# A two-layer encoder in split fp32: when ScalarE is asked for the second silu of a seven-product chunk and for the high parts of pair sums

## The chip, the core and the metric

The kernel runs on one core of a Trainium2 chip. The metric is the device time of one execution in microseconds (us); the core works on batch 1, 256 tokens, model width 1024.

## What is computed

Two layers, each `x += 0.5*SwiGLU(norm(x)); x += Mixer(norm(x)); x += 0.5*SwiGLU(norm(x))`, then a last RMSNorm. Layer 0 mixes with global and windowed attention, layer 1 with neighbourhood attention. The change touches only the four SwiGLU blocks:

```python
def swiglu(h, w_gate, w_up, w_down):          # h: 256 x 1024, d_ff = 2816
    return (jax.nn.silu(h @ w_gate) * (h @ w_up)) @ w_down
```

All in float32.

## The kernel before

Every fp32 operand of a product is split into a high part (fp32r, written by ScalarE: `high_part`, L474) and a low part (the rest, written by VectorE: `low_part`, L477). A "product" is then three TensorE matmuls (L466 to L468): high by high, low by high, high by low. Weights come in 1 MB loads into three rotating `raw` tiles; a load is asked for on the SP queue (L376) as soon as the low part of the last piece of an earlier load is asked for. Split weights live in seven `hi`/`lo` pairs (`wp`).

The four SwiGLU blocks are called stages 0, 2, 3 and 5. In each, d_ff is worked in five chunks of 512 columns and one of 256. Usually gate and up are two runs of eight products for each half (`tt`) of the 256 tokens. One or two chunks in each stage (table `SEVEN`, six in all) replace eight products by seven for some row pairs (Strassen's scheme over 2 x 2 blocks: two halves of the tokens by gate and up). Their results lie in seven or eight PSUM banks (`M["1"]`, `"5"`, `"6"`, `"7"`, `"00"`, `"01"`, `"10"`, `"11"`), and VectorE adds them up (`common`, `first_gate`, `rest` in `seven_gates`): `first_gate` gives the first half's gate and its silu (L785); `rest` gives the first half's up, then the second half's gate (L802) and its silu (L804), the second half's up (L805, L808) and the product of the two (L789, `up`).

Each finished 128 x 512 product of gate and up (`glu`) is turned by `transposed`: ScalarE copies it into two planes (L551), SP issues a transposing DMA (L553), ScalarE copies it back (L555), and the high and low parts `g_h`, `g_l` are made for the down product. Fifteen pairs of rows of the down product (the `s` entries in `DOWN`) are done by the seven-product scheme as well. For these, `quarters` copies pieces of the turned product (L696, L699) into a tile called `quarters`, which has one buffer, VectorE forms sums (L702, and L709, L710 in `sums_of`), and their high and low parts are called `k<f>h` and `k<f>l`, with `f` twice the pair's number.

Every engine takes its instructions in the order in which the Python code asks for them; no scheduler reorders them. The order of side work comes from generators: each `yield n` means "go on n products later", counted by `tick`, which runs after each product that TensorE is asked for. Supplying one more split weight (`supply`) is also counted there. So a number in a `yield` sets how many products', and thereby how many weights', instructions stand ahead on each queue.

Of the kernel before, what the change touches and what calls it, by code (L numbers as in the profile page):

```python
# [13 lines left out]
AF = mybir.ActivationFunctionType  # L14
# [39 lines left out]
R_WAIT = 3  # L54
GLU_WAIT = 6
TURN_WAIT = [1, 16]
NAT_WAIT = 2
ROPE_WAIT = [3, 3]
KB_WAIT = {
# [143 lines left out]
class Trunk:  # L203
# [343 lines left out]
    def turned_over(self, m, w):  # L547
# [3 lines left out]
        self.nc.scalar.copy(planes.rearrange("p (h c) -> p h c", h=2), back.rearrange("p (c h) -> p h c", h=2))  # L551
        yield TURN_WAIT[0]
        self.nc.sync.dma_start_transpose(back.rearrange("p (j t) -> p j t", t=P), planes)  # L553
        yield TURN_WAIT[1]
        self.nc.scalar.copy(planes.rearrange("p (c h) -> p h c", h=2), back.rearrange("p (h c) -> p h c", h=2))  # L555
# [98 lines left out]
    def ffn(self):  # L654
        nc = self.nc
# [19 lines left out]
        def transposed(tt, f0, w, m):  # L675
            n = w // P
            tb = yield from self.turned_over(m, w)
            pairs = [f for f in range(f0, f0 + n) if f in paired and f + 1 < f0 + n]
            parts = []
            for f in pairs:  # L680
                yield from quarters(tt, f, tb, f - f0)

            if tt == 1 and f0 + n - 2 in pairs:
                n -= 1
            yield from self.split_psum(tb, n, f"g{tt}_{f0}_", parts)
            for j, part in enumerate(parts):
                gT[tt][f0 + j] = part
            for f in pairs if tt == 1 else []:
                yield from sums_of(f)
# [16 lines left out]
        def sums_of(f):  # L706

            k = paired[f]
            nc.vector.tensor_tensor(k[:, 1, :], k[:, 2, :], k[:, 1, :], op=ALU.subtract)  # L709
            nc.vector.tensor_tensor(k[:, 0, :], k[:, 1, :], k[:, 0, :], op=ALU.add)  # L710
            yield 1
            hi, lo = (self.t([P, 4, P], f"k{f}{p}", 1, F32R) for p in "hl")
            self.high_part(hi, k)
            yield 1
            self.low_part(lo, k, hi)
            sums[f] = [(hi[:, i, :], lo[:, i, :]) for i in (3, 2, 1, 0)]

# [33 lines left out]
        def seven_gates(f0, w, pairs7):  # L751

            while len(K) < 4:
                self.tick(False)
            self.rate = SEVEN_RATE[self.now.n]
            h, M, c = self.now.hT, {}, {}
            op = nc.vector.tensor_tensor

            def copy():
                yield 1  # L760
                c["m"] = self.t([P, 512], "glu", 3)
                nc.scalar.activation(c["m"], M["1"], AF.Copy)

            def common():

                yield 1
                while "m" not in c:
                    yield 1
                w = self.t([P, 512], "silu", 2)
                op(w, M["6"], c["m"], op=ALU.add)  # L770
                yield 1
                y = self.t([P, 512], "glu", 3)
                op(y, M["5"], w, op=ALU.subtract)
                yield 1
                nc.vector.scalar_tensor_tensor(w, M["7"], -1.0, w, op0=ALU.mult, op1=ALU.add)
                c["y"], c["w"] = y, w

            def first_gate():
                yield 1
                while "m" not in c:  # L780
                    yield 1
                s = self.t([P, 512], "silu", 2)
                op(s, M["00"], c["m"], op=ALU.add)
                yield 1
                nc.scalar.activation(s, s, AF.Silu, scale=self.now.r[0])  # L785
                c["s"] = s

            def up(tt, o, u, s):
                nc.vector.scalar_tensor_tensor(o, u, self.now.r[tt], s, op0=ALU.mult, op1=ALU.mult)  # L789
                self.spawn(transposed(tt, f0, w, o), GLU_WAIT)  # L790
                yield 1

            def rest():
                yield 1
                while "s" not in c or "w" not in c:
                    yield 1
                y, z, m = c["y"], c["w"], c["m"]
                op(y, M["01"], y, op=ALU.add)
                yield 1
                tasks.append(self.start(up(0, y, y, c["s"])))  # L800
                yield 1
                op(m, M["10"], z, op=ALU.add)  # L802
                yield 1
                nc.scalar.activation(m, m, AF.Silu, scale=self.now.r[1])  # L804
                op(z, M["5"], z, op=ALU.subtract)  # L805
                yield 1
                if "11" in M:
                    op(z, M["11"], z, op=ALU.add)  # L808
                    yield 1
                tasks.append(self.start(up(1, m, z, m)))  # L810

            def product(name, lh, piece, first, last):
                self.mm(M[name], lh, piece, first, last)

            n7 = KD // 2 - pairs7
            M.update((name, self.bank(tag)) for name, tag in [("00", "s"), ("01", "s"), ("10", "s")])
            if n7:
                M["11"] = self.bank("o")
            for q in range(KD // 2):
                k, first, last = 2 * q, q == n7, q == KD // 2 - 1  # L820
                if q < n7:
                    pieces = self.take(4)
                    for i in range(2):
                        for n, piece in enumerate(pieces[2 * i : 2 * i + 2]):
                            for tt in range(NT):
                                product(f"{tt}{n}", h[tt][k + i], piece, k + i == 0, tt == n == 1 and i == 1 and q + 1 == n7)
                    continue
                b11, b21, b22, t7, t5, t8, t6 = self.take(7)
                if first:
                    for task in tasks:  # L830
                        self.finish(task)
                    M.update((name, self.bank(tag)) for name, tag in [("1", "pj"), ("5", "pj"), ("7", "tp")])
                    M["6"] = self.bank("tp" if n7 else "o")
                j = q - (KD // 2 - most)
                product("1", h[0][k + 1], b11, first, last)
                if last:
                    self.start(copy())
                product("00", h[0][k], b21, q == 0, last)
                if last:
                    tasks.append(self.start(first_gate()))  # L840
                product("01", K[0][j], b22, q == 0, last)
                product("7", K[3][j], t7, first, last)
                product("5", K[2][j], t5, first, last)
                product("10", h[1][k], t8, q == 0, last)
                product("6", K[1][j], t6, first, last)
            self.start(common())
            tasks.append(self.start(rest()))

        f0 = 0
# [456 lines left out]
    def odd(self, rel):  # L1306
# [11 lines left out]
        def natural(i, tt, ps, dst):  # L1318
# [7 lines left out]
            nc.scalar.activation(nat, ps, AF.Copy, scale=rs[tt] if i == 0 else r)  # L1326
            yield NAT_WAIT
            tb = self.turned(nat)
# [234 lines left out]
```

## Time and profile before

| | |
|---|---|
| median of 3 runs | 964.62 us (964.39 to 965.56) |
| the profiled execution | 964.38 us, span of its core 962.6 us |
| mean granted TensorE clock | 0.989 |
| busy: TensorE, VectorE, ScalarE, GpSimd | 931.9, 791.1, 676.4, 91.9 us |
| weight load (beside TensorE's matmuls) | 757.2 us |
| HBM | 177 GB/s over the span |

In the profile, PE is TensorE's matmul, PEld its weight load, DVE VectorE, ACT ScalarE, POOL GpSimd, SP the queue that issues the loads. A row reads `output<-inputs`, with buffer numbers left out. A bracket at the end of a timeline row gives the time that the engine stood idle ahead of it and what ended most of that. Times are from the start of the span.

### The profile page before, as it was taken

To read this page: it belongs to the slowest core of one execution; us is meant where nothing else is said; L and a number is where in the kernel's file an instruction comes from. 1 tells how busy PE (TensorE), PEld (TensorE's weight loads), DVE (VectorE), ACT (ScalarE), POOL (GpSimd) and SP (SyncE) were. 2 spreads that over 40 slices of the span, in tenths; PEclk is the share of its full clock that TensorE was granted. 3 is DMA by queue.
4 is the path that set the end of the run, shared out by engine and by line. 5 is a ranking of instruction groups with operands and counts; after the bars stand their busy time and mean duration, and the time that the engine had idled before them with its cause. 6 is when DMAs were issued, how large, how long until landed. Compare 5 with 4: busy or idle time off the path is not lost.

```text
span 962.6 us, 12408 instructions
## 1 busy us (share of the span) xinstructions
PE 931.9 (97%) x4399; PEld 757.2 (79%) x4399; DVE 791.1 (82%) x1228; ACT 676.4 (70%) x1091; POOL 91.9 (10%) x152
## 2 busy tenths in 40 slices
PE   9999999999999999999999989899999999999997
PEld 6887888877788787887887768688778788878885
DVE  6799688778879988688978887888777787986898
ACT  7687885567787686774766758647777687767763
POOL 1300000064410000000100000006130000000001
PEclk9999999999999999999999999899999999999999
DMA  8857876553246675867557567564543448477751
GB/s 298 277 153 247 263 213 215 182 138 88 89 132 197 219 213 181 244 204 262 175 141 239 171 209 225 199 242 126 174 133 131 132 144 272 121 257 218 224 208 56
DMA packets 129343, 183.16 MB, mean 190 GB/s; under 512 B 50688, under 2 KB 63744, under 8 KB 129280
## 3 DMA queue, kind: packets, MB, share of 16 engines
q1 hardware_dynamic: 128704, 181.58, 59.8%
q8 instruction: 34, 0.56, 0.2%
q10 hardware_dynamic: 576, 0.79, 0.2%
q14 instruction: 29, 0.24, 0.1%
HBM read 169.76 MB, written 1.05 MB: 177 GB/s over the span
## 4 chain that ended last, share of the span: by engine, by line
PE 48%; DVE 26%; ACT 14%; issue 6%; DMA 4%; POOL 0%; SPq 0%; POOLq 0%; ACTq 0%; DVEq 0%
DVE lo L477 10%; PE pj L466 7%; PE pj L468 7%; PE pj L467 7%; ACT hi L474 6%; PE s L467 6%; PE s L468 6%; PE s L466 5%; DVE raw L392 2%; DMA glu<-turned 2%; DVE two L392 2%; ACT turned L555 2%; DVE slo L477 2%; PE o L1035 2%; DVE g_l L477 1%
## 5 line engine op out<-in xcount | busy, mean ns | idle before, releaser
L477 DVE TENSOR_TENSOR lo<-raw,hi 128x1024 fp32r<-128x1024 f32 (+1 forms) x372 | 376.5, 1030 | 100.8 <-ACT hi L474 99.6
L474 ACT ACTIVATE hi<-raw 128x1024 fp32r<-128x1024 f32 (+1 forms) x372 | 317.6, 889 | 47.7 <-PE s L468 17.8
L467 PE MATMUL s<-lo,th 128*128 128x512 f32 x373 | 146.7, 393 | 7.9 <-DVE lo L477 7.8
L466 PE MATMUL s<-hi,th 128*128 128x512 f32 x373 | 147.0, 394 | 3.1 <-ACT hi L474 1.5
L466 PE MATMUL pj<-hi,th 128*128 128x512 f32 x367 | 147.0, 401 | 0.0
L467 PE MATMUL pj<-lo,th 128*128 128x512 f32 x367 | 143.8, 392 | 2.4 <-DVE lo L477 2.3
L468 PE MATMUL s<-hi,tl 128*128 128x512 f32 x373 | 145.9, 391 | 0.0
L468 PE MATMUL pj<-hi,tl 128*128 128x512 f32 x367 | 143.4, 391 | 0.0
L467 PEld LDWEIGHTS s<-lo,th 128*128 128x128 f32 x373 | 70.2, 188 | 25.4 <-DVE lo L477 11.5
L466 PEld LDWEIGHTS s<-hi,th 128*128 128x128 f32 x373 | 70.2, 188 | 19.4 <-ACT hi L474 3.3
L467 PEld LDWEIGHTS pj<-lo,th 128*128 128x128 f32 x367 | 69.2, 189 | 16.8 <-DVE lo L477 4.0
L468 PEld LDWEIGHTS s<-hi,tl 128*128 128x128 f32 x373 | 70.3, 188 | 14.4
L466 PEld LDWEIGHTS pj<-hi,th 128*128 128x128 f32 x367 | 69.3, 189 | 14.5 <-issue 0.9
L468 PEld LDWEIGHTS pj<-hi,tl 128*128 128x128 f32 x367 | 69.0, 188 | 14.6
L486 POOL TENSOR_TENSOR rstd<-var,mhalf 128x1 f32<-128x1 f32 (+2 forms) x16 | 17.1, 1070 | 613.5 <-ACT th L507 328.9
L555 ACT COPY turned<-glu 128x1024 uint16<-128x1024 uint16 (+1 forms) x48 | 60.1, 1253 | 10.3 <-DMA glu<-turned 10.3
L468 PE MATMUL s<-hi,g_l 128*128 128x512 f32 (+1 forms) x131 | 51.8, 396 | 3.7 <-DVE g_l L477 3.7
L551 ACT COPY turned<-glu 128x1024 uint16<-128x1024 uint16 (+1 forms) x48 | 46.2, 964 | 9.7 <-DVE glu L672 7.3
L466 PE MATMUL s<-hi,g_h 128*128 128x512 f32 (+1 forms) x131 | 52.1, 398 | 0.0
L467 PE MATMUL s<-lo,g_h 128*128 128x512 f32 (+1 forms) x131 | 51.3, 392 | 0.0
L474 ACT ACTIVATE shi<-two 128x1024 fp32r<-128x1024 f32 x30 | 31.7, 1055 | 27.0 <-DVE two L392 27.0
L477 DVE TENSOR_TENSOR slo<-raw,shi 128x1024 fp32r<-128x1024 f32 x30 | 36.6, 1220 | 11.1 <-ACT shi L474 11.1
(483 smaller groups left out, 1685.8 us busy)
## 6 DMA issues: line engine op xcount, KB each, us to landing
raw<-in_ffn_w_down SPq DMA_DIRECT2D x44, 1024.0 KB, 5.2
raw<-in_ffn_w_up SPq DMA_DIRECT2D x28, 1024.0 KB, 5.2
raw<-in_ffn_w_gate SPq DMA_DIRECT2D x26, 1024.0 KB, 5.2
raw<-in_ffn_w_gate SPq DMA_DIRECT2D x35, 512.0 KB, 4.0
raw<-in_ffn_w_up SPq DMA_DIRECT2D x32, 512.0 KB, 5.0
raw<-in_odd_w_qkv SPq DMA_DIRECT2D x12, 1024.0 KB, 5.1
raw<-in_even_w_in SPq DMA_DIRECT2D x4, 1024.0 KB, 5.2
raw<-in_even_w_out SPq DMA_DIRECT2D x8, 512.0 KB, 5.9
```

Source lines behind the costliest of these rows:

```text
L392: add = lambda o, x, y: self.nc.vector.tensor_tensor(o, x, y, op=ALU.add)
L466: mm(ps, h, wh, start=first, stop=False)
L467: mm(ps, h, wl, start=False, stop=False)
L468: mm(ps, l, wh, start=False, stop=last)
L474: self.nc.scalar.activation(hi, src, AF.Copy)
L477: self.nc.vector.tensor_tensor(lo, src, hi.bitcast(F32), op=ALU.subtract)
L486: nc.gpsimd.tensor_tensor(r[:, :n], v[:, :n], self.mhalf[:, :n], op=ALU.pow)
L551: self.nc.scalar.copy(planes.rearrange("p (h c) -> p h c", h=2), back.rearrange("p (c h) -> p h c", h=2))
L555: self.nc.scalar.copy(planes.rearrange("p (c h) -> p h c", h=2), back.rearrange("p (h c) -> p h c", h=2))
L1035: self.nc.tensor.matmul(O[64 * s : 64 * s + 64, i * P : i * P + P], v(b0 + i, s, kc), pT[s][:, i, kc, :], start=(kc == 0), stop=(kc == 1),)
```

## The change

Two lists of waits are new. In `sums_of` the high part of a pair sum is asked for six products after VectorE's sums, and the low part two after that; it was one and one. In `first_gate` the first silu is asked for three products after VectorE's sum instead of one. In `rest` the second silu (L804 before, L811 now) moves from one product behind its sum to behind the second half's up sums and four products more, and the product of the two comes another two products later.

```diff
+SUMS_WAIT = [6, 2]
+SILU_WAIT = [3, 4, 2]
...
         def sums_of(f):
...
             nc.vector.tensor_tensor(k[:, 0, :], k[:, 1, :], k[:, 0, :], op=ALU.add)
-            yield 1
+            yield SUMS_WAIT[0]
             hi, lo = (self.t([P, 4, P], f"k{f}{p}", 1, F32R) for p in "hl")
             self.high_part(hi, k)
-            yield 1
+            yield SUMS_WAIT[1]
             self.low_part(lo, k, hi)
...
                 op(s, M["00"], c["m"], op=ALU.add)
-                yield 1
+                yield SILU_WAIT[0]
                 nc.scalar.activation(s, s, AF.Silu, scale=self.now.r[0])
...
                 op(m, M["10"], z, op=ALU.add)
                 yield 1
-                nc.scalar.activation(m, m, AF.Silu, scale=self.now.r[1])
                 op(z, M["5"], z, op=ALU.subtract)
                 yield 1
                 if "11" in M:
                     op(z, M["11"], z, op=ALU.add)
-                    yield 1
+                yield SILU_WAIT[1]
+                nc.scalar.activation(m, m, AF.Silu, scale=self.now.r[1])
+                yield SILU_WAIT[2]
                 tasks.append(self.start(up(1, m, z, m)))
```

TensorE's and GpSimd's rows stand in the same order as before; on SP, at two places, a transposing DMA of a second half stands behind one weight load more. Lines below the new lists are numbered two or three higher in the changed kernel (L474 becomes L476, L804 becomes L811). Three places of the order follow.

ScalarE in stage 2, chunk 3 (the seven-product chunk whose second silu ran at 379.99 us); `hi<-raw` rows are weights, `silu_37xx` the first silu, `glu_3718` the second, `turned` the copies for turning. Before:

```order
L785 ACTIVATE silu_3731<-silu_3731,rstd_2940 128x512
L474 ACTIVATE hi_3740<-raw_3605 128x1024
L474 ACTIVATE k10h_3750<-quarters_3670 128x512
L474 ACTIVATE hi_3757<-raw_3695 128x1024
L474 ACTIVATE hi_3770<-raw_3695 128x1024
L474 ACTIVATE hi_3791<-raw_3711 128x1024
L804 ACTIVATE glu_3718<-glu_3718,rstd_3030 128x512
L667 ACTIVATE silu_3812<-pj_3764,rstd_2940 128x512
L551 COPY turned_3821<-glu_3780 128x1024
L474 ACTIVATE hi_3823<-raw_3711 128x1024
L474 ACTIVATE hi_3836<-raw_3747 128x1024
L551 COPY turned_3846<-glu_3718 128x1024
```

and in the changed kernel:

```order
L476 ACTIVATE hi_3739<-raw_3600 128x1024
L787 ACTIVATE silu_3731<-silu_3731,rstd_2940 128x512
L476 ACTIVATE hi_3753<-raw_3695 128x1024
L476 ACTIVATE hi_3766<-raw_3695 128x1024
L476 ACTIVATE k10h_3781<-quarters_3670 128x512
L476 ACTIVATE hi_3790<-raw_3711 128x1024
L669 ACTIVATE silu_3810<-pj_3760,rstd_2940 128x512
L553 COPY turned_3819<-glu_3776 128x1024
L476 ACTIVATE hi_3821<-raw_3711 128x1024
L811 ACTIVATE glu_3718<-glu_3718,rstd_3030 128x512
L476 ACTIVATE hi_3835<-raw_3746 128x1024
L476 ACTIVATE hi_3846<-raw_3746 128x1024
```

The first silu moved behind one weight's high part, k10's high part behind two more, and the second silu from ahead of the next chunk's first silu (`silu_38xx`) to behind it, the first half's turning copy and one more high part; the second half's turning copy left this stretch.

ScalarE in stage 3, where the second half of the first seven-product chunk is copied back and its pair sum k6 is split; `shi` rows are the high parts of weights of seven-product pairs. Before:

```order
L555 COPY turned_5032<-glu_4910 128x2x512
L551 COPY turned_5132<-glu_5083 128x1024
L699 ACTIVATE quarters_5104<-turned_5032 128x128
L474 ACTIVATE g_4_h_5147<-turned_5032 128x384
L474 ACTIVATE shi_5152<-two_5116 128x1024
L474 ACTIVATE k6h_5165<-quarters_5104 128x512
L474 ACTIVATE shi_5168<-raw_5015 128x1024
L474 ACTIVATE hi_5178<-raw_5041 128x512
L474 ACTIVATE hi_5189<-raw_5041 128x1024
L551 COPY turned_5199<-glu_5150 128x1024
L474 ACTIVATE shi_5201<-two_5185 128x1024
```

and in the changed kernel:

```order
L553 COPY turned_5131<-glu_5083 128x1024
L476 ACTIVATE shi_5146<-two_5116 128x1024
L476 ACTIVATE shi_5156<-raw_5013 128x1024
L557 COPY turned_5061<-glu_4910 128x2x512
L476 ACTIVATE hi_5166<-raw_5039 128x512
L701 ACTIVATE quarters_5104<-turned_5061 128x128
L476 ACTIVATE hi_5178<-raw_5039 128x1024
L476 ACTIVATE g_4_h_5186<-turned_5061 128x384
L553 COPY turned_5195<-glu_5144 128x1024
L476 ACTIVATE shi_5197<-two_5173 128x1024
L476 ACTIVATE k6h_5220<-quarters_5104 128x512
```

The copy back of `glu_4910` moved behind two `shi` rows, and k6's high part from ahead of a chunk's last `shi` to behind the first `shi` of the next load.

ScalarE in stage 3's down product, around the pair sum k16. Before:

```order
L474 ACTIVATE hi_5669<-raw_5511 128x512
L699 ACTIVATE quarters_5625<-turned_5560 128x128
L474 ACTIVATE g_16_h_5685<-turned_5560 128x512
L474 ACTIVATE k16h_5697<-quarters_5625 128x512
L474 ACTIVATE hi_5700<-raw_5511 128x1024
L555 COPY turned_5610<-glu_5572 128x2x256
L474 ACTIVATE shi_5718<-two_5676 128x1024
```

and in the changed kernel:

```order
L476 ACTIVATE hi_5669<-raw_5511 128x512
L701 ACTIVATE quarters_5625<-turned_5556 128x128
L476 ACTIVATE g_16_h_5685<-turned_5556 128x512
L476 ACTIVATE hi_5697<-raw_5511 128x1024
L557 COPY turned_5610<-glu_5568 128x2x256
L476 ACTIVATE shi_5714<-two_5676 128x1024
L476 ACTIVATE k16h_5722<-quarters_5625 128x512
```

k16's high part moved behind a weight's high part, a copy back and one `shi`.

## Prediction

> **What bounds the kernel now.** First the page (busy time by engine), then the list of waits, which says who keeps whom waiting (total us, times, longest).
>
> ```profile
> PE 931.9 (97%) x4399; PEld 757.2 (79%) x4399; DVE 791.1 (82%) x1228; ACT 676.4 (70%) x1091; POOL 91.9 (10%) x152
> ...
> ACT glu L804 <- DVE glu L802: 30.4, 6, 6.2
> ...
> PE s L467 <- DVE lo L477: 7.8, 8, 2.0
> ...
> ACT k16h L474 <- DVE quarters L710: 10.8, 3, 4.2
> ```
>
> TensorE (PE) is busy 97% of the span, so the most that a new order can return are its few gaps. The longest of them end with a low part of a weight (`lo`, L477), which VectorE makes out of the high part from ScalarE. ScalarE meanwhile stands 30.4 us at the six second silus (L804), some 5 us each, for VectorE's sum at L802. These ScalarE waits cost nothing by themselves; what counts is whether the weights queued behind them come late. I name the six chunks with seven products by the time of their L804: A 84.61, B 333.77, C 379.99, D 517.86, E 568.21, F 853.81. The timeline around A shows the chain (start, duration, in brackets the idle time and what ended it):
>
> ```profile
> 84.61 0.72 ACT L804 ACTIVATE glu<-glu,rstd 128x512 f32<-128x512 f32 x1 [5.51 <-DVE glu L802]
> ...
> 88.79 1.23 DVE L477 TENSOR_TENSOR lo<-raw,hi 128x1024 fp32r<-128x1024 f32 x1 [0.58 <-ACT hi L474]
> ...
> 88.64 0.40 PE L468 MATMUL s<-hi,tl 128*128 128x512 f32 x1
> 88.87 0.44 PE L466 MATMUL s<-hi,th 128*128 128x512 f32 x1
> 90.07 0.50 PE L467 MATMUL s<-lo,th 128*128 128x512 f32 x1 [0.76 <-DVE lo L477]
> ```
>
> ScalarE stood 5.51 us, its next high parts came late, VectorE waited for one of them (0.58), and TensorE for the low part. Matmuls start 0.23 us apart when nothing is missing (88.64, 88.87); here the next started after 1.20, so TensorE lost 0.97, which is the bracket plus 0.2. I use "bracket plus 0.2" below.
>
> **The change, chunk by chunk.** No instruction is added or taken away and TensorE's order is the same. On ScalarE the second silu (0.72) and the first one move behind later high parts; the second half's last product (L789, 0.75) moves behind one or two low parts on VectorE; its turning copy, its transposing DMA and its copy back follow some 2 to 4 us later; the high and low parts of the pair sums move behind three to six products' worth of weights.
>
> *A.* The high parts that stood behind L804 now stand ahead of it, so VectorE's idle 0.58 goes and L789 (0.75) stands behind the low part: it is 1.3 us early against a wait of 0.97. Gain 1.0.
>
> *B.* TensorE waits for nothing there; no gain. The cover is that its low parts were in time already; were it gone, one wait like A's, 1.0, would come.
>
> *C.* Two waits of TensorE lie here.
>
> ```profile
> 379.99 0.72 ACT L804 ACTIVATE glu<-glu,rstd 128x512 f32<-128x512 f32 x1 [5.84 <-DVE glu L802]
> 382.12 2.00 ACT L474 ACTIVATE hi<-raw 128x1024 fp32r<-128x1024 f32 x2
> ...
> 370.81 1.23 DVE L477 TENSOR_TENSOR lo<-raw,hi 128x1024 fp32r<-128x1024 f32 x1 [0.75 <-ACT hi L474]
> 381.51 0.75 DVE L789 SCALAR_TENSOR_TENSOR glu<-silu,rstd,glu 128x512 f32<-128x512 f32 x1
> 383.21 2.36 DVE L477 TENSOR_TENSOR lo<-raw,hi 128x1024 fp32r<-128x1024 f32 x2 [0.95 <-ACT hi L474]
> ...
> 372.09 0.51 PE L467 MATMUL pj<-lo,th 128*128 128x512 f32 x1 [0.76 <-DVE lo L477]
> 383.24 0.49 PE L466 MATMUL s<-hi,th 128*128 128x512 f32 x1 [0.19 <-ACT hi L474]
> 384.49 0.50 PE L467 MATMUL s<-lo,th 128*128 128x512 f32 x1 [0.76 <-DVE lo L477]
> ```
>
> At 372.09 the low part waited 0.75 for a high part queued behind the first silu. That silu now stands one high part later, so 0.75 of the 0.97 comes back. At 383.24 and 384.49 TensorE lost 0.35 and 0.97. The low part there is now early by the idle 0.95, L789's 0.75 and the 0.75 from above, 2.45 in all, while TensorE comes at most 0.75 earlier; both waits go. Gain 0.75 + 1.3 = 2.1.
>
> *D and E, one stage.* This is the largest term, and here a later wait takes part of the gain back.
>
> ```profile
> 522.37 0.50 PE L467 MATMUL s<-lo,th 128*128 128x512 f32 x1 [0.77 <-DVE lo L477]
> 547.64 0.50 PE L467 MATMUL s<-lo,th 128*128 128x512 f32 x1 [1.86 <-DVE lo L477]
> 551.85 0.63 PE L467 MATMUL s<-slo,th 128*128 128x512 f32 x1
> 565.92 0.47 PE L466 MATMUL s<-hi,th 128*128 128x512 f32 x1 [1.49 <-DVE glu L798]
> 571.45 0.50 PE L466 MATMUL s<-hi,th 128*128 128x512 f32 x1 [1.17 <-ACT hi L474]
> 572.71 0.71 PE L467 MATMUL s<-lo,th 128*128 128x512 f32 x1 [0.76 <-DVE lo L477]
> 618.02 0.80 PE L468 MATMUL s<-hi,g_l 128*128 128x512 f32 x1 [3.69 <-DVE g_l L477]
> ...
> 539.83 0.63 ACT L474 ACTIVATE k6h<-quarters 128x512 fp32r<-128x512 f32 x1 [3.59 <-DVE quarters L710]
> 568.21 0.73 ACT L804 ACTIVATE glu<-glu,rstd 128x512 f32<-128x512 f32 x1 [6.18 <-DVE glu L802]
> 579.26 1.36 ACT L555 COPY turned<-glu 128x1024 uint16<-128x1024 uint16 x1 [1.01 <-DMA glu<-turned]
> 604.99 0.63 ACT L474 ACTIVATE k16h<-quarters 128x512 fp32r<-128x512 f32 x1 [4.15 <-DVE quarters L710]
> ...
> 541.44 1.22 DVE L477 TENSOR_TENSOR slo<-raw,shi 128x1024 fp32r<-128x1024 f32 x1 [1.71 <-ACT shi L474]
> 549.26 1.23 DVE L477 TENSOR_TENSOR slo<-raw,shi 128x1024 fp32r<-128x1024 f32 x1
> 606.60 1.23 DVE L477 TENSOR_TENSOR lo<-raw,hi 128x1024 fp32r<-128x1024 f32 x1 [1.71 <-ACT hi L474]
> 617.55 0.42 DVE L477 TENSOR_TENSOR g_l<-turned,g_h 128x256 fp32r<-128x256 f32 x1
> ...
> 573.10 4.92 SPq L553 DMA_TRANSPOSE glu<-turned  x2
> ```
>
> Two of these waits are followed by a stretch at half clock. Rows of the view by stretches (length, PE busy, PEld, DVE, ACT, POOL, then the granted clock):
>
> ```profile
> 454.50:457.60 3.10, 1.81 (x9) 1.16 (x8) 3.03 (x6) 0.00 (x0) 0.00 (x0) 1.00 0.59 229
> 545.53:548.94 3.41, 1.55 (x8) 1.08 (x7) 3.38 (x5) 3.38 (x5) 0.00 (x0) 1.00 0.96 273
> 548.94:552.36 3.42, 3.42 (x10) 2.64 (x9) 3.42 (x4) 3.42 (x4) 0.00 (x0) 0.50 0.18 26
> ```
>
> After 3.41 us with 1.55 busy the next 3.4 us ran at 0.50. One such stretch costs about 1.6 (eight starts 0.43 instead of 0.23 apart), and one follows 547.64 and one 572.71. I count TensorE's lead and VectorE's lead apart, since the smaller rules at 618.02.
>
> TensorE: 522.37 is A's case again: 1.0. Its low part, and so the next load and what hangs on it, comes some 1.7 early (C's 0.95 and 0.75). At 539.83 ScalarE stood 3.59 for a pair sum, the shifted high parts behind it came late, and VectorE idled 1.71. Those high parts now stand ahead of it; with the 1.7 from above the low part that ended the 547.64 wait is over 3 us early, so 2.0 and the 1.6 of half clock go. But the pair sum now stands ahead of the last shifted part of that chunk, which gains only the 1.7; TensorE, 4.6 early, waits there anew. By the slack before (the part done at 550.49, used at 551.85) that is 4.6 - 1.7 - 1.4 = 1.5. Lead 1.0 + 2.0 + 1.6 - 1.5 = 3.1. At 565.92 it waited for the bank that L798 empties; the sums ahead of it lose a pair sum's high and low part and one silu, about 2.3, and are 4.0 early: lead 4.0. At 571.45 and 572.71 TensorE waited for a weight queued behind L804's 6.18; by the 4.0 and the terms of C its low part is about 5.2 early: lead 5.2, and 6.8 with the half clock gone.
>
> VectorE: that same low part frees the buffer of the load behind which the transposing DMA of 573.10 is issued; it landed at 579.26, 6.2 later, so the chain that runs from there to 618 starts 5.2 early. On this chain the pair sum k12 gives something back: `quarters` has one buffer, and its copy for the next chunk (L696) now has to wait until k12's low part, which stands behind another low part (1.22 as at 541.44), is done; I take 1.5 of idle, between 0 and 2. k16 gives: the 1.71 idle at 606.60 goes, since the high part no longer stands behind the 4.15 wait. 5.2 - 1.5 + 1.7: the `g_l` of 617.55 comes 5.4 early. TensorE, 6.8 early, waits longer there, 5.3 instead of 3.9, and runs at half clock behind it as before. Gain of the stage: 5.4. Its ends are 1.7 (only k16's idle returned) and 6.8 (the chain keeps pace).
>
> *F and the end.*
>
> ```profile
> 858.32 0.50 PE L467 MATMUL s<-lo,th 128*128 128x512 f32 x1 [0.72 <-DVE lo L477]
> 946.23 0.50 PE L467 MATMUL o<-lo,g_h 128*128 128x512 f32 x1 [0.17 <-DVE lo L477]
> ...
> 889.51 0.63 ACT L474 ACTIVATE k14h<-quarters 128x512 fp32r<-128x512 f32 x1 [2.35 <-DVE quarters L710]
> ...
> 898.32 1.23 DVE L477 TENSOR_TENSOR lo<-raw,hi 128x1024 fp32r<-128x1024 f32 x1 [0.46 <-ACT hi L474]
> ```
>
> 858.32 is A's case: 0.9. From 898.32 VectorE works almost without a gap to the end, and TensorE waits for it a little (0.3 at 946.23 and some 0.1s). That row starts about 2 us earlier when k14h no longer holds ScalarE 2.35, so 0.5 comes back there, and the 0.9 is kept.
>
> What moves late costs nothing by my reckoning: the second halves are read in the down product, over 20 us behind their chunk, and the pair sums later still. On SP the second transposing DMA of A and E moves behind one load (0.4 of issue, and the wait for that load's buffer); nothing behind it is due sooner. GpSimd's row doesn't move.
>
> **Sum.** 1.0 + 0 + 2.1 + 5.4 + 0.9 + 0.5 = 9.9 us. The profiled execution took 964.38 (span 962.6 and 1.8 around it), 0.24 under the median of 964.62; 964.4 - 9.9 = 954.5.
>
> **Rivals.** *The gain is taken back at 618.* If the chain to 618 starts no earlier, because a load's landing and not the low part holds its start, the stage gives 1.7 instead of 5.4: 958.2. For it: the row at 579.26 waits for a DMA, 6.2 us after its issue. Against: that issue followed the low part of 572.71 within 0.5.
>
> *The half clock stays.* If the two half-clock stretches aren't due to the waits of 2.0, TensorE's lead is 6.8 - 3.2 = 3.6, which then rules, and the sum is 8.1: 956.3. Against it stand the rows: 1.55 of 3.41 busy was followed by 0.50, and the 1.81 of 3.10 at 454.50 shows that a wait of 1.3 leaves the clock alone. [...]
>
> *Nothing changes.* ScalarE's waits (30.4 at L804, 10.8 at k16 alone) just move to other rows, and VectorE, busy 82%, still sets each low part: 964.4. Against: each of the waits above has an idle VectorE ahead of it that ends with a high part.
>
> *Slower.* The second half's transposing DMA lands so late that ScalarE, which works in order, stands at the copy back with weights behind it. Before, it stood 1.01 at 579.26 for the first half. The landing takes some 6 us and the copy back has about 3 us of slack by the new order. If it were over 2 us later than that in all six chunks, each would cost TensorE a wait of 2.0 and half clock of 1.6: 21.6 - 9.9, so 976.1. It decides from about three chunks on.
>
> **How the numbers follow.** Forecast 0.55, with its own range of 951 to 957; taken back at 618: 0.19; half clock stays: 0.12; nothing: 0.07; slower: 0.07. 0.2% (1.9 us) is about what a measurement of this kernel can tell from no change. Faster 0.86, same 0.07, slower 0.07. The range 951.0 to 959.5 leaves out the last two cases and little else: its low end is the sum with 6.8 for the stage and one half-clock stretch (1.6) fewer behind 618, its high end the first rival with A's and F's terms at a third.
>
> **What would show it.** In the profile after: no wait of over 1 us at L811 (the new L804); no PE bracket behind A, C, D and F's second silus; no half clock near 547 and 572; a longer wait for `g_l` near 610, ending some 8.5 us earlier than 618.02 (5.4 and A's and C's 3.1); a wait of the `quarters` copy for k12's low part. I would be wrong if ScalarE waited at the second copies back, or if the wait near 610 ended less than 6 us early.

## The result, and the profile after

The changed kernel takes 948.99 us (median of 4 runs, 948.73 to 950.02); the kernel before, on the same chip, 964.50 (4 runs, 963.44 to 965.56). The ratio is 0.9841 (95% interval 0.9824 to 0.9858): 15.5 us are gone, where 9.9 were forecast, and the time lies 2 us below the low end of the range. The profiled execution took 949.13, with a span of 947.3 against 962.6.

The first line of the page of after, to be held against the first one of before: TensorE is busy 7.0 us less, though it does the same work. So 8.3 of the 15.3 us of span were idle time, and the rest is matmuls that lasted longer, above all at half clock (0.63 us each at 551.42 of before, 0.39 at 552.55, where the clock is full again).

```profile
PE 924.9 (98%) x4399; PEld 755.3 (80%) x4399; DVE 789.6 (83%) x1228; ACT 678.6 (72%) x1091; POOL 90.8 (10%) x152
```

The list of waits of after no longer has the 30.4 us at the second silu. What stands there of its kind (the first row is the two silus, one for each half, of the chunk behind a seven-product chunk; each of these waits is shorter than the one at L804 was):

```profile
ACT silu L669 <- DVE glu L791: 20.1, 10, 4.9
...
ACT turned L557 <- DMA glu<-turned: 6.1, 7, 2.1
...
ACT k16h L476 <- DVE quarters L712: 3.8, 3, 1.8
ACT k6h L476 <- DVE quarters L712: 2.9, 1, 2.9
...
ACT quarters L698 <- DVE k12l L479: 2.5, 1, 2.5
```

TensorE issues the same matmuls in the same order in both kernels, so each of its rows of before has one partner. These are the partners, in the timeline of after (start, duration, in brackets the idle time and what ended it), of the rows shown for before:

```profile
88.89 0.39 PE L469 MATMUL s<-lo,th 128*128 128x512 f32 x1
...
369.87 0.50 PE L469 MATMUL pj<-lo,th 128*128 128x512 f32 x1
380.66 0.39 PE L468 MATMUL s<-hi,th 128*128 128x512 f32 x1
380.88 0.39 PE L469 MATMUL s<-lo,th 128*128 128x512 f32 x1
452.06 0.60 PE L524 MATMUL tp<-mats,x 128*128 128x128 f32 x4
515.42 0.39 PE L469 MATMUL s<-lo,th 128*128 128x512 f32 x1
538.54 0.39 PE L469 MATMUL s<-lo,th 128*128 128x512 f32 x1
541.63 0.49 PE L468 MATMUL s<-shi,th 128*128 128x512 f32 x1 [0.44 <-ACT shi L476]
542.89 0.50 PE L469 MATMUL s<-slo,th 128*128 128x512 f32 x1 [0.77 <-DVE slo L479]
545.59 0.50 PE L468 MATMUL pj<-hi,th 128*128 128x512 f32 x1 [1.27 <-ACT glu L764]
556.64 0.39 PE L468 MATMUL s<-hi,th 128*128 128x512 f32 x1
560.72 0.39 PE L468 MATMUL s<-hi,th 128*128 128x512 f32 x1
561.53 0.50 PE L469 MATMUL s<-lo,th 128*128 128x512 f32 x1 [0.43 <-DVE lo L479]
606.37 0.50 PE L470 MATMUL s<-hi,g_l 128*128 128x512 f32 x1 [3.65 <-DVE g_l L479]
844.56 0.39 PE L469 MATMUL s<-lo,th 128*128 128x512 f32 x1
...
931.60 0.39 PE L469 MATMUL o<-lo,g_h 128*128 128x512 f32 x1
```

A row's start before minus its start after is TensorE's lead; a jump in it is a gain at that place. Nearly all brackets of before are gone. The row at 452.06 is new here: it is the first transpose of stage 3, and before it had a bracket of its own, which the prediction did not look at:

```profile
457.60 0.44 PE L522 MATMUL tp<-mats,x 128*128 128x128 f32 x2 [1.29 <-DVE x L609]
```

| place (before / after) | lead | gained since the row above | forecast |
|---|---|---|---|
| A: 90.07 / 88.89 | 1.18 | 1.2 | 1.0 |
| C: 384.49 / 380.88 | 3.61 | 2.4 | 2.1 |
| border of stages 2 and 3: 457.60 / 452.06 | 5.54 | 1.9 | 0 |
| 547.64 / 538.54 | 9.10 | 3.6 | 3.0 |
| the third new wait: 553.24 / 545.59 | 7.65 | -1.5 | 1.6 of half clock less 1.5 |
| 572.71 / 561.53 | 11.18 | 3.5 | 2.1 |
| g_l: 618.02 / 606.37 | 11.65 | 0.5 | stage in all 5.4 |
| F: 858.32 / 844.56 | 13.76 | 2.1, of it 0.9 at F | 0.9 |
| 946.23 / 931.60 | 14.63 | 0.9 | 0.5 |

ScalarE and VectorE at the two places where the prediction expected something to be given back:

```profile
537.78 0.63 ACT L476 ACTIVATE k6h<-quarters 128x512 fp32r<-128x512 f32 x1 [2.91 <-DVE quarters L712]
538.32 1.34 ACT L557 COPY turned<-glu 128x1024 uint16<-128x1024 uint16 x1
540.54 1.04 ACT L476 ACTIVATE shi<-raw 128x1024 fp32r<-128x1024 f32 x1
...
584.81 0.42 ACT L698 ACTIVATE quarters<-turned 128x256 f32<-128x256 f32 x1 [2.52 <-DVE k12l L479]
...
586.14 0.48 DVE L674 SCALAR_TENSOR_TENSOR glu<-s,rstd,silu 128x256 f32<-128x256 f32 x1 [1.43 <-ACT silu L669]
```

And the clock, in the view by stretches (length, busy time of PE, PEld, DVE, ACT, POOL, then the granted clock, the share of the DMA engines and GB/s):

```profile
314.30:317.71 3.41, 1.45 (x8) 0.84 (x6) 3.34 (x5) 2.17 (x3) 0.00 (x0) 1.00 0.92 297
317.71:321.12 3.41, 3.41 (x8) 2.73 (x9) 3.41 (x4) 3.41 (x5) 0.00 (x0) 0.50 0.10 17
601.02:604.43 3.41, 1.70 (x8) 1.05 (x6) 3.34 (x5) 1.26 (x2) 0.00 (x0) 1.00 0.96 382
604.43:607.85 3.42, 1.48 (x6) 1.24 (x7) 3.42 (x5) 3.03 (x4) 0.00 (x0) 1.00 0.57 223
607.85:611.26 3.41, 3.41 (x9) 2.65 (x8) 3.41 (x4) 2.04 (x3) 0.00 (x0) 0.50 0.40 108
```

Before the last stage's end, the profile of before had five stretches of 3.41 us at half clock (320, 549, 573 and two from 617); after has two (317.71 and 607.85). The row of 601.02 has TensorE busy for 1.70 us and no half clock behind it.

### The profile page after: what moved, and what is told of

It is laid out like the page before. It is cut to its first block, busy times and chain, and to the rows that moved or that the text cites. A ratio compares the mean times of both kernels' runs of the same rounds, so it can differ in the third digit from the quotient of the medians.

```text
span 947.3 us, 12407 instructions
## 1 busy us (share of the span) xinstructions
PE 924.9 (98%) x4399; PEld 755.3 (80%) x4399; DVE 789.6 (83%) x1228; ACT 678.6 (72%) x1091; POOL 90.8 (10%) x152
## 4 chain that ended last, share of the span: by engine, by line
PE 72%; DVE 15%; ACT 6%; issue 4%; DMA 2%; POOL 0%; SPq 0%; POOLq 0%; ACTq 0%; DVEq 0%
PE s L469 10%; PE s L470 10%; PE s L468 10%; PE pj L468 9%; PE pj L469 9%; PE pj L470 9%; DVE lo L479 6%; PE o L470 2%; PE o L469 2%; PE o L468 2%; ACT hi L476 2%; PE o L1038 2%; DVE raw L394 1%; DVE two L394 1%; PE tp L1117 1%
## 5 line engine op out<-in xcount | busy, mean ns | idle before, releaser
L476 ACT ACTIVATE hi<-raw 128x1024 fp32r<-128x1024 f32 (+1 forms) x372 | 319.3, 889 | 54.5 <-PE s L470 16.7
L476 ACT ACTIVATE shi<-two 128x1024 fp32r<-128x1024 f32 x30 | 31.7, 1057 | 26.2 <-DVE two L394 26.1
L476 ACT ACTIVATE shi<-raw 128x1024 fp32r<-128x1024 f32 x30 | 31.7, 1056 | 23.9 <-PE s L470 13.0
```

The source lines that it names most:

```text
L476: self.nc.scalar.activation(hi, src, AF.Copy)
```

## The experiments

**e1: the silus alone.** In the changed kernel, pair sums as before.

```diff
-SUMS_WAIT = [6, 2]
+SUMS_WAIT = [1, 1]
```

> The changed kernel with the pair sums' high and low parts one and one product behind their sums, as before; only the silus stay moved. Theory K (the 1.55 us that TensorE gained at the border of stages 2 and 3 come from stage 2's pair sum k16): A 1.3 and C 2.4 stay, the 1.44 of wait at the first transposes of stage 3 are back in full; in stage 3 VectorE is some 5.2 early by D and E, and TensorE's wait for g_l near 610 ends by that much earlier; F 0.9, end 0.3. Sum 10.1, 954.4 us (953 to 956). Theory S (the border's 1.55 come from the silus of C, whose low parts are over 2 us early): the wait at the border is gone, 952.8 us (951.5 to 954).

**e2: the pair sums alone.** In the kernel before:

```diff
-            yield 1
+            yield SUMS_WAIT[0]       # 6
             ...
-            yield 1
+            yield SUMS_WAIT[1]       # 2
             self.low_part(lo, k, hi)
```

> The kernel before with the pair sums' high and low parts six and two products behind their sums; the silus stay where they were. Theory K: no gain at A, C and F, the border's wait is gone (1.55 early behind 458); the wait of 2.0 near 547 goes with its half clock, but TensorE is held near 541 to 546 and for g_l near 615, where VectorE gains 1.7 by k16 and loses 1.4 by the wait for quarters; end 0.5. Sum 1.55 + 0.3 + 0.5 = 2.4 (up to 4 where a half-clock stretch falls away), 962.1 us (960 to 962.5). Theory S: the border's wait stays; 0.3 + 0.5, 963.6 us (962.5 to 964.4).

**e3: all but stage 2's k16**, and **e4: stage 2's k16 alone.** The waits are chosen by stage and pair; e3 in the changed kernel, e4 in the kernel before.

```diff
+            wait = [1, 1] if (self.now.n, f) == (2, 16) else SUMS_WAIT     # e3
+            wait = [6, 2] if (self.now.n, f) == (2, 16) else [1, 1]        # e4
```

> The changed kernel, with only stage 2's pair sum k16 back at one and one product. Theory K: ScalarE waits some 4 us at k16h again, the loads of stage 2's last third are asked for some 3 us later, the wait of 1.3 to 1.5 at the first transposes of stage 3 is back, and all that follows is 1.55 later: 950.5 us (950.0 to 951.2). Theory S: same as the changed kernel, 949.0 us (948.6 to 949.4).

> The kernel before, with only stage 2's pair sum k16 six and two products behind its sums. Theory K: the wait at the border falls away, TensorE and VectorE are both 1.5 early in stage 3, and it is kept to the end: 963.0 us (962.5 to 963.4). If VectorE had been the later of the two only at that one place and had no lead of its own, the wait for g_l at 618 takes it all back: 964.4 us. Theory S: the border's wait stays, 964.4 us (964.0 to 964.8).

The four shared one chip and 15 runs of the kernel before (median 963.89).

| | median us | ratio (95%) | near 318 / 549 / 573 / the g_l | 
|---|---|---|---|
| e1 | 952.70 (4 runs) | 0.9885 (0.9872 to 0.9899) | 0 / 0 / 0 / 2 |
| e2 | 953.97 (5 runs) | 0.9899 (0.9882 to 0.9915) | 0 / 2 / 0 / 0 |
| e3 | 948.10 (5 runs) | 0.9846 (0.9829 to 0.9863) | 0 / 0 / 0 / 2 |
| e4 | 962.33 (11 runs) | 0.9988 (0.9979 to 0.9998) | 1 / 0 / 1 / 1 |

The last column counts the half-clock stretches of 3.41 us in the profiled execution; before has 1 / 1 / 1 / 2. The first transpose of stage 3 in each (e1, e2, e3, e4), and ScalarE's row of stage 2's k16 in e1 and in e4:

```profile
451.28 0.38 PE L524 MATMUL tp<-mats,x 128*128 128x128 f32 x2
```

```profile
455.17 0.38 PE L523 MATMUL tp<-mats,x 128*128 128x128 f32 x2
```

```profile
450.26 0.38 PE L524 MATMUL tp<-mats,x 128*128 128x128 f32 x2
```

```profile
456.10 0.38 PE L522 MATMUL tp<-mats,x 128*128 128x128 f32 x2
```

```profile
412.00 0.63 ACT L476 ACTIVATE k16h<-quarters 128x512 fp32r<-128x512 f32 x1 [4.16 <-DVE quarters L712]
```

```profile
418.86 0.64 ACT L474 ACTIVATE k16h<-quarters 128x512 fp32r<-128x512 f32 x1 [0.34 <-DVE quarters L711]
```

No bracket stands in any of the four, so both theories on the border fall as stated: K, since e1 and e3 keep ScalarE's 4.2 us at k16h and still have no wait at the border; S, since e4 leaves C's silus where they were and has none either. Either part alone makes VectorE early enough. Before, its last addition for this transpose (L609) ended 1.3 us after TensorE was ready; TensorE's time can only be won once. The time of e3, within the interval of the changed kernel's, says the same.

What it is worth is another matter. No run has the border's wait together with the rest of the change, so its worth in the changed kernel is read from leads alone. In e4 TensorE is 1.5 us early at the border, but the g_l near 617 comes only 0.96 us early (617.06 against 618.02), and that much is kept. The profiled execution, 2.2 us shorter than that of before, has the other 1.2 from the clock: one half-clock stretch behind the g_l instead of two.

E1 came out at S's number, for another reason; the size expected for e2 was off by 8 us. The two gains, 11.2 and 9.9, add up to 21, well over the changed kernel's 15.5: they overlap. The g_l ends 9.6 us early in e1, 7.2 in e2 and 11.7 in both together; in e1 and e2 some 1.6 of this is the half-clock stretch near 318, which their executions don't have and those of before and after have. The border counts in both, and so do some of TensorE's brackets:

| TensorE's bracket in before at | before | e1, silus alone | e2, sums alone |
|---|---|---|---|
| A: 90.07 | 0.76 | 0 | 0.53 |
| C: 372.09 and 384.49 | 0.76, 0.76 | 0, 0 | 0.76, 0.76 |
| D: 522.37 | 0.77 | 0 | 0.75 |
| 547.64 | 1.86 | 0 | 0 |
| E: 565.92, the bank | 1.49 | 1.44 | 0 |
| E: 571.45 | 1.17 | 0.04 | 0 |
| E: 572.71 | 0.76 | 0.76 | 0 |
| F: 858.32 | 0.72 | 0.29 | 0.02 |

At A, C and D the silus make the gain, as predicted. At E it is mostly the pair sums: in e2 ScalarE still stands at E's second silu, and TensorE's partner of 572.71 has no bracket.

```profile
563.70 0.72 ACT L805 ACTIVATE glu<-glu,rstd 128x512 f32<-128x512 f32 x1 [5.65 <-DVE glu L803]
...
568.21 0.50 PE L468 MATMUL s<-lo,th 128*128 128x512 f32 x1
```

For e2 I had left out that k6's and k10's sums no longer hold ScalarE in stage 3 (3.6 and 1.5 us before, none in e2), though the rows for it were there.

**e5: the wait for `quarters`.**

```diff
-                paired[f] = self.t([P, 4, P], "quarters")
+                paired[f] = (self.t([P, 4, P], "quarters") if (self.now.n, f) != (3, 16)
+                             else self.t([P, 4 * P], "silu", 2).rearrange("p (a b) -> p a b", b=P))
```

> The changed kernel; stage 3's pair sum k16 gets its quarters in a spare buffer of another tile, so that their first copy (584.81 in the changed kernel, 2.52 us of wait behind k12's low part) waits for nothing. Theory W (this wait is on VectorE's path to the g_l near 606): VectorE's idle 1.43 at 586.14 goes, the wait for g_l ends 1.4 earlier, 947.6 us (946.5 to 948.3), give or take 1.6 for one stretch at half clock more or less. Theory L (VectorE has work or a load to wait for there in any case): the idle time moves to the next row and the time stays 949.0 us (948.5 to 949.8).

945.32 us (4 runs), 0.9809 (0.9792 to 0.9827). The g_l in e5 and, for comparison, in e3:

```profile
602.85 0.50 PE L470 MATMUL s<-hi,g_l 128*128 128x512 f32 x1 [2.49 <-DVE g_l L479]
```

```profile
604.32 0.80 PE L470 MATMUL s<-hi,g_l 128*128 128x512 f32 x1 [3.65 <-DVE g_l L479]
```

The wait ends 3.5 us earlier than in the changed kernel. VectorE is 1.4 ahead already at k12's low part, which stands before the buffer (582.61 against 584.04), mostly because this execution, like e3's (granted clock 1.00 from 313.14 to 323.38), has no half clock near 318; the other 2.1 are the buffer's. Theory W holds, with 2.1 for 1.4: VectorE loses 1.4 at the idle time, and 0.6 more a few rows on, where it stands 0.79 for a high part in the changed kernel (590.30) and 0.22 in e5. E5 to e8 shared a second chip with 9 runs of the kernel before (median 963.88), e9 and e10 a third with 9 (963.70).

**e6: TensorE's new waits at 541 to 546.** The copy back of the second chunk's first half and k6's split are asked for six products later.

```diff
+            late = 22 if (self.now.n, f0, tt) == (3, 8, 0) else TURN_WAIT[1]     # 16
+            wait = [12, 2] if (self.now.n, f) == (3, 6) else SUMS_WAIT
```

> The changed kernel; in stage 3 the copy back of the second chunk's first half (538.32) and k6's split are asked for six products later, so that ScalarE makes the high part shi (540.54) in the 2.9 us in which it waits for k6's sum. All theories: TensorE's waits at 541.63, 542.89 and 545.59 (3.07 us in all) go or shrink below 1. Theory V (behind them VectorE's chain to the g_l near 606 sets the end): TensorE comes 3 us early, waits 6 to 7 us for g_l instead of 3.8, and the time stays 949.0 us, with one or two half-clock stretches of 1.6 more or less behind that wait (948 to 951). Theory T (TensorE's lead also frees weights, buffers and loads earlier, and VectorE follows): 946.0 us (945 to 947).

947.98 us (5 runs), 0.9837 (0.9818 to 0.9855): the same as the changed kernel within the interval.

```profile
543.18 0.58 ACT L765 ACTIVATE glu<-pj 128x512 f32<-128x512 f32 x1
...
543.81 0.50 PE L468 MATMUL pj<-hi,th 128*128 128x512 f32 x1 [3.03 <-ACT glu L765]
604.34 0.79 PE L470 MATMUL s<-hi,g_l 128*128 128x512 f32 x1 [3.68 <-DVE g_l L479]
```

The first two waits went, the third did not: TensorE comes earlier to a bank that ScalarE empties (L765) behind two copies, and stands 3.03 instead of 1.27 there, with a half-clock stretch behind it (mean granted clock 0.994, 0.996 in after). The common expectation, that all three would go or shrink below 1, failed on that point. Theory V holds: the g_l ends at 604.34, as in e3 (604.32), whether TensorE waits at 541 or not. The new waits at this place, 1.5 in the prediction, measure 2.5 by the brackets and 3.1 with 0.2 for each, and they cost nothing, since VectorE's chain sets the end. They don't come from the pair sums' new waits: e1, which has the old ones, shows 0.95, 0.76 and 1.27 there.

**e7: g_l ahead of the sums.** VectorE makes the g_l of 606 behind three sums for the next seven-product pair.

```diff
+            late = 14 if (self.now.n, f0, tt) == (3, 20, 1) else TURN_WAIT[1]    # 16
+            tb = yield from self.turned_over(m, w, late)
```

> The changed kernel; in stage 3 the last chunk's second half is copied back two products earlier, so that its g_l stands ahead of VectorE's sums for the next seven-product pair (602.17 to 604.84) instead of behind them. Theory G (the g_l is only asked for too late; VectorE has what comes next ready in time: the low part of 604.76 is first used 4.6 us behind the wait): the wait of 3.8 goes with its half-clock stretch of 1.6, 943.6 us (942.5 to 945.5). Theory B (VectorE itself is behind, and this wait only shows it first): TensorE waits about as long for the next low parts and for the split weights behind them, 948.5 us (947 to 949.5).

943.35 us (4 runs), 0.9796 (0.9775 to 0.9817). The g_l, and what is late next:

```profile
600.80 0.39 PE L470 MATMUL s<-hi,g_l 128*128 128x512 f32 x1
634.00 0.47 PE L524 MATMUL tp<-mats,x 128*128 128x128 f32 x1 [2.21 <-DVE x L611]
```

The 3.65 are gone and no low part is late behind them: theory G. Of theory B this much shows, that VectorE is late again 33 us on: TensorE waits 2.21 us at the border of stages 3 and 4. The three runs without a profile took 943.25 to 943.42; the profiled one 946.58, with a half-clock stretch behind that new wait (633.74 to 637.15, granted clock 0.50).

**e8: e6 and e7 together.**

> The changed kernel with both edits of stage 3: the copy back and k6 six products later, the last chunk's second half two products earlier. Theories V and G: with the wait for g_l gone, TensorE's 3 us from 541 to 546 are kept, 943.6 - 3.0 = 940.6 us (939.5 to 942.5). Theories V and B: as the second edit alone, since VectorE sets the end of the stage, 948 us (946.5 to 949.5).

944.48 us (4 runs), 0.9797 (0.9779 to 0.9815): as e7 within the interval, and in neither of the expected ranges. The 3 us of 541 to 546 are not kept even with the g_l in time, so the number of V and G together failed. TensorE still waits 2.89 for the bank at 545.03, and 1.78 at the next border, where VectorE's last additions set the end. The 948 of V and B did not come either; e7 alone had shown G.

**e9: e7 with e5's buffer**, the fastest version of all.

> The kernel of the earlier g_l (the last chunk's second half copied back two products earlier) with the spare buffer for stage 3's k16 as well. In the first, TensorE stands 2.37 us at the first transposes of stage 4 (634.00) for VectorE's last additions; in the second, VectorE is 1.4 us earlier in the same down product. Theory V (VectorE's chain now sets the end of stage 3, and the 1.4 reach it): that wait falls to about 1.0, below what halves the clock, 943.35 - 1.4 = 942.0 us (941.0 to 943.0). Theory L (VectorE waits for ScalarE's high parts at the end of the stage in any case, as the 1.25 of idle ahead of 628.80 say): the wait stays, 943.4 us (943.0 to 945).

942.96 us (5 runs, 942.04 to 943.27), 0.9775 (0.9755 to 0.9795).

```profile
632.69 0.33 PE L524 MATMUL tp<-mats,x 128*128 128x128 f32 x1 [0.38 <-DVE x L611]
```

The wait at the border falls from 2.21 to 0.38: theory V's mechanism. The time is at the upper end of what it gave, and its interval overlaps e7's; the profiled execution has a half-clock stretch near 318, which e7's has not (its mean granted clock is 0.996; the two executions at 0.999 took 942.04 and 942.29).

**e10: the first silu back.**

```diff
-SILU_WAIT = [3, 4, 2]
+SILU_WAIT = [1, 4, 2]
```

> The changed kernel with the first silu of the seven-product chunks back at one product behind its sum; the second silu and the pair sums stay moved. Theory P (the first silu's place is worth 0.75 at C, and as much to VectorE in stage 3): the wait of 0.97 near 370 is back, and the wait for g_l near 606 ends 0.75 later still: 950.5 us (949.8 to 951.3). Theory N (the first silu's move does nothing; the wait near 370 went because the second silu and the pair sums moved): 949.0 us (948.5 to 949.7).

950.07 us (4 runs), 0.9850 (0.9829 to 0.9871).

```profile
371.25 0.50 PE L469 MATMUL pj<-lo,th 128*128 128x512 f32 x1 [0.76 <-DVE lo L479]
608.25 0.50 PE L470 MATMUL s<-hi,g_l 128*128 128x512 f32 x1 [3.69 <-DVE g_l L479]
...
603.00:606.41 3.41, 1.56 (x7) 0.94 (x6) 3.34 (x5) 1.26 (x2) 0.00 (x0) 1.00 0.98 400
606.41:609.83 3.42, 1.58 (x7) 1.32 (x8) 3.42 (x5) 2.97 (x4) 0.00 (x0) 1.00 0.50 199
609.83:613.24 3.41, 3.41 (x17) 2.81 (x16) 3.41 (x4) 2.01 (x2) 0.00 (x0) 1.00 0.50 131
```

The bracket of 0.76 near 370 is back to the hundredth, and the g_l is 1.9 later than in the changed kernel. Of this 0.4 is lost in the first 62 us, ahead of every seven-product chunk, 0.84 at 371.25 and most of the rest from 517 to 544: theory P, with 1.5 for its 1.5. The time alone would not tell, since its interval overlaps the changed kernel's. In the profiled executions only 0.3 of the 1.9 is left at the end, mostly because here no half clock follows the wait for g_l.

## Why the prediction was right or wrong

*Direction and mechanism: right in the main.* No wait at L811 is left among the longer ones, no bracket behind the second silus of A, C, D and F, no half clock at 547 and 572, and the copy of `quarters` waits for k12's low part. One sign did not come: the wait for g_l is not longer but the same (3.65 for 3.69, where 5.3 with the 0.2 was forecast).

*A, C, F, the end: right in size, or a little small.* 1.2, 2.4, 0.9 and 0.9 against 1.0, 2.1, 0.9 and 0.5. E10 shows C's first part by itself: the first silu, 0.75 forecast, 0.84 measured. F is not wholly "A's case again": with the silu in place and only the sums moved (e2), 0.02 of its 0.72 is left, with the silus alone (e1) 0.29.

*The border of stages 2 and 3: the step that failed.* "What moves late costs nothing" and the list of six chunks took stage 2's down product for a place without a gain, though the page of before names ScalarE's 4.2 us at a k16h and the timeline has TensorE's 1.29 at 457.60. Its removal gave 1.5 there (the lead goes from 4.09 one row earlier to 5.54), and either part of the change does it alone (e1, e4).

*D and E: the term was mis-sized.* The g_l ended 11.65 earlier, not 8.5. TensorE came into the stage 5.5 early instead of 3.1, and the stage gave 6.1 for the 5.4 forecast: most of the difference was there before the stage began, 1.9 of it since C, with the border. That VectorE's chain inherits this lead is read from the rows and not isolated; in e4 0.96 of 1.5 reached the g_l. Inside, errors cancelled: k16 gave 1.8 (1.7 forecast); k12's wait for the buffer took 2.1 for 1.5 (e5); TensorE's new waits were 3 for 1.5, and free, since VectorE ruled (e6). The cause given for E's brackets at 571.45 and 572.71, a weight queued behind the second silu's 6.18, was at most a part of it: the sums alone clear both, and the one at 565.92, while the silus alone clear only 571.45's. That VectorE's chain and not TensorE's lead decides at the g_l was right, and e7 shows it directly; but TensorE was not a further 1.4 ahead there, as forecast (its lead one row before the wait is 11.61).

*"Runs at half clock behind it as before": wrong for this execution.* One stretch instead of two followed, worth 1.23 us. E1 and e3 had two behind the same wait, e10 none. The term should have been a range from 0 to 2 stretches; the low end allowed one fewer and left out the border. Its own terms come to 951.5, not 951.0 (964.4 less 11.3 and 1.6); with the border's 1.9 since C it would have been 949.6. The last 0.6 is several small differences: A, C and the end gave 0.2 to 0.4 more each, the stage 0.7 less than the low end's 6.8, the half clock 0.4 less than its 1.6, and 0.7 more came behind 946.23.

*The rivals.* "Taken back at 618" did not happen: the chain started early with its low part. "Nothing changes" was right in that ScalarE's waits moved on, to the next chunk's two silus (20.1 for 30.4 us, the longest 4.9); but only one matmul behind them came late, E's at 561.53, by 0.43 for 0.76. "The half clock stays", to which I gave 0.12 as an estimate, fell at 549 and 573. The length of a wait alone did not tell: one of 1.96 was followed by half clock at 317.71, and one of 3.69 in e10 was not. "Slower" did not show: ScalarE's waits for a transposing DMA before the copy back come to 6.1 us in seven places, none over 2.1.

## What to carry to other kernels

An engine that works in order should not be asked for a step until the step's input is due: of the six second silus at which ScalarE stood 3 to 6 us, five had a late weight one or two engines on (B's had none), and four of the late weights, A, C, D and a part of F, left with the silus alone. When such waits are taken away, look for every place where the slower engine's lead is spent, also at stage borders where the list of waits shows only one short bracket. And ask what is late next: one buffer (e5) and one copy back asked for two products earlier (e7) were worth 2 and about 5 us more, while removing 3 us of waits off the deciding chain (e6) gave nothing.

## What the runs showed of the hardware

The cost of a wait in half clock depended on where it fell. In the profiles of before and after all half-clock stretches start on one grid of 3.413 us (before: 548.94 - 320.25 is 67 of them, 617.21 - 548.94 is 20; after: 607.85 - 317.71 is 85), and the grid lies elsewhere in each execution (its stretches near 318 start at 316.84 in before, 317.71 in after, 316.28 in e10). Of the stretches of the grid that ran at full clock in before and after, from 10 us on, those in which TensorE was busy for 1.55 us or less were followed by one at half clock, and those with 1.70 or more were not. One at half clock cost some 1.2 to 1.6 (after's lead grows by 1.23 behind the g_l, where it has one stretch and before two; eight starts are 0.43 instead of 0.23 apart in the stretch behind 547.64).

The same wait of 3.65 to 3.69 for g_l was followed by two stretches in the kernel before, e1, e3 and e6, by one in after and e4, and by none in e10, where it was cut in halves of 1.56 and 1.58 busy. The wait of 2 us near 318, which no kernel here takes away (1.99 in before, 1.96 in after), was followed by half clock in before, after and e10, where the stretch ahead had 1.42, 1.45 and 1.51 busy, and not in e3, where the grid cut it into stretches of 2.36 and 2.48. Over all runs the busy time does not part the cases as cleanly as in before and after: in e2 two waits of 0.81 and 0.76 (546.58 and 547.84), which leave 1.84 of 3.41, were followed by half clock, and in e10 the 1.56 and 1.58 were not.

So two executions of one kernel can differ by a few us (e7: 943.25 to 943.42 at a mean granted clock of 0.998, 946.58 at 0.996), and a difference of 1.5 us between two kernels is read from the leads in the trace before it is read from the times. The kernel before ranged from 960.45 to 967.89 over the three chips of the experiments. Its slower executions tend to have the lower mean granted clock (on the chip of e1 to e4 the five slowest of 15 had 0.989 to 0.992, the five fastest 0.992 to 0.997), but half clock is not all of it: on one chip, executions with the same 0.994 took 962.18 to 965.14.
